# Gate products of a recurrent branch in two 64-row halves of TensorE, with ScalarE moving the input gates between halves

## The chip, the core and the metric

The kernel runs on one core of a Trainium2 chip. The metric is the device time of one execution in microseconds (us). TensorE (PE) multiplies a stationary matrix (`lhsT`, at most 128 rows by 128 columns) with a moving one and accumulates in PSUM; PEld is its loading of the stationary matrix. ScalarE (ACT), VectorE (DVE) and GpSimd (POOL) work element by element, and SyncE (SP) issues most of the transfers.

## The reference

A trunk of two layers on 256 positions of 1024 channels. Each layer mixes tokens by three branches (dilated attention, a gated linear recurrence, retention) and then retrieves experts. The change concerns the gates of the recurrence, `lx` being 1024 of the columns of the input projection:

```python
xc = lax.conv_general_dilated(lx, conv_w[:, None, :], ..., feature_group_count=LRU_WIDTH) + conv_b
xr = xc.reshape(B, S, LRU_BLOCKS, LRU_BLOCK_DIM)                       # 16 blocks of 64 channels
r = jax.nn.sigmoid(jnp.einsum('bsgi,gio->bsgo', xr, wa).reshape(B, S, C) + ba)
i = jax.nn.sigmoid(jnp.einsum('bsgi,gio->bsgo', xr, wx).reshape(B, S, C) + bx)
a = jnp.exp(-LRU_C * r * jax.nn.softplus(-lam))
b = jnp.sqrt(-jnp.expm1(2.0 * log_a)) * (i * xc)                        # h_t = a_t h_(t-1) + b_t
```

Both gate matrices are block diagonal: 16 blocks of 64 by 64, so a tile of 128 channels holds two blocks.

## The kernel before

All weights stream through the core as **jobs**: a job is one tile of 128 by 1024 float32. For each, SP loads `raw` (L220), ScalarE casts it to the high part `wh` (L239) and VectorE subtracts to get the low part `wl` (L256), so that three fast products (`xh` by `wh`, `xl` by `wh`, `xh` by `wl`) stand for one exact product. `run` works job by job: it first issues cast and subtraction of the job two ahead (`ensure_split(i + LA)`, `LA = 2`), then the products of job i (`body`), then a share of side work (`pump`), then what follows the job (`post`). Each engine executes in this order of issue.

The jobs of a layer are numbered here from 0: 0 to 7 give `lx` (a job is 24 products of 256 columns, with `wl` in the last eight, L307), 8 to 19 give the attention values `av` (12 products of 512 columns, L343, L344, L347, with `wl` from the fifth on), 20 to 43 the attention's queries and keys, and so on. After every second `lx` job, `post` copies the finished pair to `lx` in SBUF (L650, or L648 in layer 1's first pair); after jobs 11, 15 and 19, `post` copies `av` (L679, two copies).

Side work is written as generators whose yields are prices; `pump` resumes one while it has credit, and each job adds 1.4. The recurrence is one such queue ("lru"):

- `lru1`, once for each pair of channel tiles, four times in a layer. Two convolutions on VectorE (L583, L586), each priced 1.7. Then for each of the two tiles q a **gate group**: two products in full float32 (L594 and L595, each of which appears in the trace as two passes), two Tanh out of PSUM (L597, L598), a Tanh that makes log a (L599), and on VectorE the input gate times the convolution (L601), priced 0.5.
- `lru2`, once. Eight small operations (L610, L611), a square root over everything on ScalarE (L613), eight times a reciprocal on VectorE (L615) with two products on GpSimd, and eight times a product and a scan on VectorE (L620, L621).

The gate weights `wg` hold, for each gate and channel tile, a 128 by 128 matrix with two blocks on its diagonal and zeros elsewhere. Products of 64 rows exist elsewhere in the kernel: the attention scores (L710) multiply rows 0 to 63 and rows 64 to 127 alternately, each half into a PSUM bank of its own.

Of the kernel before, what the change touches and what calls it, by code (L numbers as in the profile page):

```python
# [11 lines left out]
F32 = mybir.dt.float32  # L12
# [3 lines left out]
AF = mybir.ActivationFunctionType  # L16
ALU = mybir.AluOpType
AX = mybir.AxisListType

S = 256  # L20
D = 1024
P = 128
KT = D // P
LAYERS = 2
# [139 lines left out]
def build(ctx: ExitStack, tc: tile.TileContext, I, out, layers=LAYERS, dbg=None):  # L164
    nc = tc.nc
    mm = nc.tensor.matmul
# [8 lines left out]
    par = cp.tile([P, LAYERS, 8, 12], F32, name="par")  # L175
# [7 lines left out]
    def nm(s):  # L183
        uid[0] += 1
        return f"{s}_{uid[0]}"
# [4 lines left out]
    def sideps():  # L190
        return ps.tile([P, 512], F32, tag="side", name=nm("side"), bufs=2)
# [364 lines left out]
    def mixer(l, mp, xdram, xnext):  # L556
        rope = mp.tile([P, 4, S], F32, name=nm("rope"), tag="rope")
        mask = mp.tile([P, 1152], F32, name=nm("mask"), tag="cst")
        wg = mp.tile([P, 2, 8, P], F32, name=nm("wg"), tag="L8", bufs=7)
        if l == 0:  # L560
            add_side("lru", init_lru(mp))

        def L8(shape=(P, 8, S), dt=F32):
            return mp.tile(list(shape), dt, tag="L8", name=nm("L8"), bufs=7)

        def w2():
            return mp.tile([P, 512], F32, tag="w2", name=nm("w2"), bufs=6)

        def pr(ct, k):
            return par[:, l, ct, k:k + 1]  # L570

        tT = L8()
        gi = L8()
# [3 lines left out]
        def lru1(c, lx):  # L577
            xcs = []
            for q in range(2):
                ct = 2 * c + q  # L580
                src = lx[:, q * S:(q + 1) * S]
                xc = mp.tile([P, S], F32, tag="xc", name=nm("xc"), bufs=3)
                nc.vector.tensor_scalar(xc, src, pr(ct, 3), pr(ct, 4), op0=ALU.mult, op1=ALU.add)  # L583
                for k in (2, 1, 0):
                    sh = 3 - k
                    nc.vector.scalar_tensor_tensor(xc[:, sh:], src[:, :S - sh], pr(ct, k), xc[:, sh:],  # L586
                                                   op0=ALU.mult, op1=ALU.add)
                xcs.append(xc)
                yield 1.7
            for q in range(2):  # L590
                ct = 2 * c + q
                xc = xcs[q]
                pg = sideps()
                mm(pg[:, 0:S], lhsT=wg[:, 0, ct, :], rhs=xc, start=True, stop=True)  # L594
                mm(pg[:, S:2 * S], lhsT=wg[:, 1, ct, :], rhs=xc, start=True, stop=True)  # L595
                tr = w2()
                nc.scalar.activation(tr[:, 0:S], pg[:, 0:S], AF.Tanh, bias=pr(ct, 5), scale=0.5)  # L597
                nc.scalar.activation(tr[:, S:2 * S], pg[:, S:2 * S], AF.Tanh, bias=pr(ct, 6), scale=0.5)  # L598
                nc.scalar.activation(tT[:, ct, :], tr[:, 0:S], AF.Tanh, bias=csp[:, l, ct:ct + 1],  # L599
                                     scale=csp[:, l, ct:ct + 1])  # L600
                nc.vector.scalar_tensor_tensor(gi[:, ct, :], tr[:, S:2 * S], 1.0, xc, op0=ALU.add, op1=ALU.mult)  # L601
                yield 0.5

        def lru2():
            sq = L8()
# [294 lines left out]
        m = L8((P, 2, D))  # L900
# [419 lines left out]
def inputs_for(x, w_in, conv_w, conv_b, lru_wa, lru_ba, lru_wx, lru_bx, lru_lambda, w_branch, w_out,  # L1320
# [11 lines left out]
    vecs = [ch(cw[:, k]) for k in range(4)] + [ch(a) for a in (conv_b, lru_ba, lru_bx, lru_lambda,  # L1332
                                                                        ln1_g, ln1_b, ln2_g, ln2_b)]
    A["par"] = f(np.stack(vecs, -1).transpose(2, 0, 1, 3))
    wg = np.zeros((LAYERS, P, 2, 8, P), np.float32)
    for m, w in enumerate((f(lru_wa), f(lru_wx))):
        for b in range(16):
            ct, o = divmod(b, 2)
            wg[:, o * 64:o * 64 + 64, m, ct, o * 64:o * 64 + 64] = w[:, b]
    A["wgate"] = wg  # L1340
    A["keys"] = f(np.stack([f(peer_k1), f(peer_k2)], 1).transpose(0, 4, 1, 2, 3))
    for n, a in (("ln1_g", ln1_g), ("ln1_b", ln1_b), ("ln2_g", ln2_g), ("ln2_b", ln2_b)):
# [18 lines left out]
```

## Time and profile before

| | us |
|---|---|
| median of the runs | 2494.98 |
| lowest | 2494.91 |
| the profiled execution | 2493.72 |
| its span, first to last instruction | 2491.9 |

| engine | busy us | share of the span |
|---|---|---|
| TensorE, products | 2464.3 | 99% |
| TensorE, loads of weights | 2245.0 | 90% |
| VectorE | 1834.6 | 74% |
| ScalarE | 1176.6 | 47% |
| GpSimd | 206.6 | 8% |

Products overlap in the pipeline, so the busy time of TensorE is not its time at peak. What a product costs in a stream is read from the distance between the starts of two neighbours.

### The profile page before, as it was taken

The page shows a single profiled execution, that of the slowest core. Times are in us where ns is not written, and L with a number is a line of the kernel's source. Part 1 is how long each engine was busy: PE and PEld are TensorE (multiplying, and loading weights), DVE is VectorE, ACT ScalarE, POOL GpSimd, SP SyncE. Part 2 cuts the span into 40 slices and gives each one's busy share as a digit, 9 for nine tenths or more (in the row PEclk, how much of TensorE's full clock was granted, in tenths as well). Part 3 has the DMA queues.
Part 4 walks back from the last instruction along what each step waited for, and adds up shares of the span by engine and source line. Part 5 has one row for each costly group of instructions (what it writes and reads, how often), then busy time and mean ns, then how long its engine had stood idle before and what let it go on. Part 6 is the DMA issues. An engine that isn't in the chain of part 4 may idle for free.

```text
span 2491.9 us, 41185 instructions
## 1 busy us (share of the span) xinstructions
PE 2464.3 (99%) x16404; PEld 2245.0 (90%) x16404; DVE 1834.6 (74%) x2732; ACT 1176.6 (47%) x1463; POOL 206.6 (8%) x195
## 2 busy tenths in 40 slices
PE   8999999999999999999999999999999999999998
PEld 7999988999999988888789999879999999888886
DVE  7976655889888856765679666578988888566656
ACT  5444444444444444444464444444454444444444
POOL 0512110100000000000015120110000000000000
PEclk9999999999999999999999999999999999999999
DMA  6544565655556558676565455656555565677664
GB/s 225 176 153 160 169 208 177 204 178 171 185 192 202 194 194 260 227 228 228 178 205 174 156 166 169 227 167 208 177 178 181 193 202 195 201 255 227 228 241 140
DMA packets 165904, 485.82 MB, mean 195 GB/s; under 512 B 15056, under 2 KB 47952, under 8 KB 165072
## 3 DMA queue, kind: packets, MB, share of 16 engines
q1 hardware_dynamic: 119952, 434.43, 53.2%
q10 hardware_dynamic: 44800, 45.62, 5.6%
q8 instruction: 129, 2.11, 0.3%
q0 software_dynamic: 960, 3.15, 0.3%
q14 instruction: 63, 0.52, 0.1%
HBM read 462.16 MB, written 20.97 MB: 194 GB/s over the span
## 4 chain that ended last, share of the span: by engine, by line
PE 97%; DVE 2%; issue 0%; ACT 0%; DMA 0%; POOL 0%; SPq 0%; ACTq 0%; DVEq 0%
PE acc L1259 28%; PE mm L304 15%; PE mm L305 15%; PE mm L307 15%; PE acc L343 6%; PE acc L344 6%; PE acc L347 6%; PE acc L1185 1%; PE acc L1186 1%; PE side L710 1%; PE side L1025 1%; PE side L766 0%; DVE wl L256 0%; PE acc L1250 0%; PE side L759 0%
## 5 line engine op out<-in xcount | busy, mean ns | idle before, releaser
L256 DVE TENSOR_TENSOR wl<-raw,wh 128x1024 fp32r<-128x1024 f32 (+1 forms) x811 | 1004.7, 1243 | 478.5 <-ACT wh L239 475.8
L239 ACT CAST wh<-raw 128x1024 fp32r<-128x1024 f32 (+1 forms) x817 | 851.7, 1050 | 639.7 <-PE acc L1259 343.1
L304 PE MATMUL mm<-xh,wh 128*128 128x256 f32 x3144 | 781.7, 286 | 0.0
L305 PE MATMUL mm<-xl,wh 128*128 128x256 f32 x3144 | 771.0, 283 | 0.0
L304 PEld LDWEIGHTS mm<-xh,wh 128*128 128x128 f32 x3144 | 602.5, 192 | 3.1 <-issue 2.6
L305 PEld LDWEIGHTS mm<-xl,wh 128*128 128x128 f32 x3144 | 603.3, 192 | 0.5
L1259 PE MATMUL acc<-wh,act 128*128 128x512 f32 x2016 | 539.3, 389 | 0.9 <-ACT act L351 0.9
L1259 PEld LDWEIGHTS acc<-wh,act 128*128 128x128 f32 x2016 | 378.4, 188 | 79.8 <-ACT act L351 1.3
L307 PE MATMUL mm<-xh,wl 128*128 128x256 f32 x3144 | 441.0, 283 | 0.0
L307 PEld LDWEIGHTS mm<-xh,wl 128*128 128x128 f32 x3144 | 405.6, 192 | 0.0
L1259 PE MATMUL acc<-wl,act 128*128 128x512 f32 x1008 | 310.2, 389 | 0.0
L1259 PEld LDWEIGHTS acc<-wl,act 128*128 128x128 f32 x1008 | 189.3, 188 | 39.2
L1228 ACT ACTIVATE ring<-mm 128x512 f32<-128x512 f32 x128 | 76.6, 599 | 189.6 <-PE mm L307 178.3
L343 PE MATMUL acc<-wh,xh 128*128 128x512 f32 x416 | 166.0, 399 | 0.0
L344 PE MATMUL acc<-wh,xl 128*128 128x512 f32 x416 | 162.3, 390 | 0.0
L347 PE MATMUL acc<-wl,xh 128*128 128x512 f32 x416 | 128.3, 390 | 0.0
L381 POOL TENSOR_TENSOR lnv<-lnv,mhalf 128x1 f32<-128x1 f32 x8 | 4.5, 558 | 1371.8 <-DVE lnv L378 1371.1
L1155 ACT ACTIVATE ge<-acc 128x512 f32<-128x512 f32 x64 | 38.4, 600 | 164.0 <-PE acc L1186 164.0
L343 PEld LDWEIGHTS acc<-wh,xh 128*128 128x128 f32 x416 | 78.2, 188 | 16.7 <-ACT r L853 0.7
L347 PEld LDWEIGHTS acc<-wl,xh 128*128 128x128 f32 x416 | 78.1, 188 | 16.7
L344 PEld LDWEIGHTS acc<-wh,xl 128*128 128x128 f32 x416 | 78.2, 188 | 15.5
L352 DVE TENSOR_TENSOR act<-ring,act 128x512 fp32r<-128x512 f32 x128 | 87.6, 685 | 3.8 <-ACT act L351 3.8
(245 smaller groups left out, 2225.9 us busy)
## 6 DMA issues: line engine op xcount, KB each, us to landing
raw<-in_ws SPq DMA_DIRECT2D x815, 512.0 KB, 3.4
gd<-ge ACTq DMA_DIRECT2D x64, 256.0 KB, 3.4
ring<-gd ACTq DMA_DIRECT2D x8, 2048.0 KB, 15.2
wg<-in_wgate SPq DMA_DIRECT2D x2, 1024.0 KB, 7.0
xd<-L POOLq DMA_DIRECT2D x8, 256.0 KB, 4.3
kk<-in_keys ACTq DMA_DIRECT2D x2, 1024.0 KB, 5.5
X<-xd ACTq DMA_DIRECT2D x2, 1024.0 KB, 5.8
dec<-in_dec ACTq DMA_DIRECT2D x2, 768.0 KB, 5.5
```

What stands on the lines that cost most here:

```text
L239: nc.scalar.copy(h[:, c], raw[:, c])
L256: e.tensor_tensor(lo[:, c], raw[:, c], h[:, c].bitcast(F32), op=ALU.subtract)
L304: mm(o, lhsT=w, rhs=mh[:, koff + k, :], start=(k == 0), stop=False)
L305: mm(o, lhsT=w, rhs=ml[:, koff + k, :], start=False, stop=False)
L307: mm(o, lhsT=lo[:, base + k * P:base + (k + 1) * P], rhs=mh[:, koff + k, :], start=False, stop=(k == n - 1))
L343: mm(acc[t], lhsT=sh[:, k, ts], rhs=h[:, q * 512:(q + 1) * 512], start=first, stop=False)
L344: mm(acc[t], lhsT=sl[:, k, ts], rhs=h[:, q * 512:(q + 1) * 512], start=False, stop=False)
L347: mm(acc[t], lhsT=sh[:, k, ts], rhs=lo[:, q * 512:(q + 1) * 512], start=False, stop=(last and q == 1))
L352: nc.vector.tensor_tensor(lo, src, h.bitcast(F32), op=ALU.subtract)
L1155: nc.scalar.activation(ge, pg.rearrange("p (k i) -> p i k", k=8)[:, 64:128, :], AF.Copy, scale=1.0 / GSCALE)
L1228: nc.scalar.activation(ring[s][:, i - 1:i + 1, :], pt.rearrange("p (a t) -> p a t", a=2), AF.Gelu)
L1259: mm(V["y"][t][n], lhsT=a[:, part, q, ts], rhs=w[:, n * 512:(n + 1) * 512], start=(j == 0 and x == 0), stop=False)
```

## The change

For a pair of channel tiles, the change makes four products of 64 rows by 128 columns (L596) where there were four of 128 by 128. Half b of the rows holds block b of a channel tile; its stationary matrix has that block of both gates side by side, so one product gives the recurrence gate and the input gate of the block. The output of half b goes to a PSUM bank of its own (`pg[b]`). In it, the recurrence gate of block b stands at the rows of block b, and the input gate at the rows of the other half. So the Tanh that reads an input gate writes to the other half (g against o in the diff), and each Tanh covers 64 rows: four for a channel tile where there were two. The two products with the convolution move behind a yield of their own, and the yields of `lru1` add up to 5.9 where they were 4.4. `wg` is half as large, and `xc` has four buffers for three.

```diff
-        wg = mp.tile([P, 2, 8, P], F32, name=nm("wg"), tag="L8", bufs=7)
+        wg = mp.tile([P, 8, P], F32, name=nm("wg"), tag="L8", bufs=7)
...
-                xc = mp.tile([P, S], F32, tag="xc", name=nm("xc"), bufs=3)
+                xc = mp.tile([P, S], F32, tag="xc", name=nm("xc"), bufs=4)
...
+            pg = [sideps(), sideps()]
+            for q in range(2):
+                for b in range(2):
+                    o = slice(64 * b, 64 * b + 64)
+                    mm(pg[b][:, q * S:(q + 1) * S], lhsT=wg[o, 2 * c + q, :], rhs=xcs[q][o, :], start=True, stop=True)
+            trs = []
             for q in range(2):
                 ct = 2 * c + q
-                xc = xcs[q]
-                pg = sideps()
-                mm(pg[:, 0:S], lhsT=wg[:, 0, ct, :], rhs=xc, start=True, stop=True)
-                mm(pg[:, S:2 * S], lhsT=wg[:, 1, ct, :], rhs=xc, start=True, stop=True)
                 tr = w2()
-                nc.scalar.activation(tr[:, 0:S], pg[:, 0:S], AF.Tanh, bias=pr(ct, 5), scale=0.5)
-                nc.scalar.activation(tr[:, S:2 * S], pg[:, S:2 * S], AF.Tanh, bias=pr(ct, 6), scale=0.5)
+                trs.append(tr)
+                for m in range(2):
+                    for b in range(2):
+                        o = slice(64 * b, 64 * b + 64)
+                        g = slice(64 * (b ^ m), 64 * (b ^ m) + 64)
+                        nc.scalar.activation(tr[o, m * S:(m + 1) * S], pg[b][g, q * S:(q + 1) * S], AF.Tanh,
+                                             bias=par[o, l, ct, 5 + m:6 + m], scale=0.5)
                 nc.scalar.activation(tT[:, ct, :], tr[:, 0:S], AF.Tanh, bias=csp[:, l, ct:ct + 1],
                                      scale=csp[:, l, ct:ct + 1])
-                nc.vector.scalar_tensor_tensor(gi[:, ct, :], tr[:, S:2 * S], 1.0, xc, op0=ALU.add, op1=ALU.mult)
-                yield 0.5
+            yield 1.5
+            for q in range(2):
+                nc.vector.scalar_tensor_tensor(gi[:, 2 * c + q, :], trs[q][:, S:2 * S], 1.0, xcs[q], op0=ALU.add,
+                                               op1=ALU.mult)
+            yield 1.0
```

Lines behind the change stand 12 later in the changed kernel (L608 is the Tanh of L599, L691 the copy of L679, L627 the reciprocal of L615, L725 the score scaling of L713).

On TensorE, layer 0, right behind job 4, the gate products of the first pair (side is the PSUM bank, xc the convolved tile):

```order
-L594 MATMUL side_344<-xc_270,wg_130 128x256
-L595 MATMUL side_344<-xc_270,wg_130 128x256
-L594 MATMUL side_352<-xc_305,wg_130 128x256
-L595 MATMUL side_352<-xc_305,wg_130 128x256
+L596 MATMUL side_344<-xc_270,wg_130 128x256
+L596 MATMUL side_345<-xc_270,wg_130 128x256
+L596 MATMUL side_344<-xc_305,wg_130 128x256
+L596 MATMUL side_345<-xc_305,wg_130 128x256
```

There are as many products as before, of the same number of moving columns, and neighbours now write to different banks. The later groups also change place: in layer 0 they stood behind jobs 7, 10 and 11, 13 and 14, and stand behind jobs 8, 12 and 17; in layer 1 they stood behind jobs 6, 9 and 12, and stand behind jobs 7, 11 and 15, which are jobs that `post` copies follow.

On ScalarE, layer 1, the third group of the change, with the cast of job 13 ahead of it and that of job 14 behind:

```order
L239 CAST wh_12987<-raw_12918 128x1024
L606 ACTIVATE w_1944_13009<-side_13003,par 64x256
L606 ACTIVATE w_1944_13009<-side_13004,par 64x256
L606 ACTIVATE w_1944_13009<-side_13003,par 64x256
L606 ACTIVATE w_1944_13009<-side_13004,par 64x256
L608 ACTIVATE L_1881_12602<-w_1944_13009,csp 128x256
L606 ACTIVATE w_1945_13015<-side_13003,par 64x256
L606 ACTIVATE w_1945_13015<-side_13004,par 64x256
L606 ACTIVATE w_1945_13015<-side_13003,par 64x256
L606 ACTIVATE w_1945_13015<-side_13004,par 64x256
L608 ACTIVATE L_1881_12602<-w_1945_13015,csp 128x256
L691 COPY av_13021<-acc_12924 128x512 x2
```

Before, the same place on ScalarE, with the copies of `av`, one cast, and then a gate group:

```order
L679 COPY av_13005<-acc_12907 128x512 x2
L239 CAST wh_13010<-raw_12925 128x1024
L597 ACTIVATE w_1954_13030<-side_13027,par 128x256
L598 ACTIVATE w_1954_13030<-side_13027,par 128x256
L599 ACTIVATE L_1881_12586<-w_1954_13030,csp 128x256
L597 ACTIVATE w_1956_13038<-side_13035,par 128x256
L598 ACTIVATE w_1956_13038<-side_13035,par 128x256
L599 ACTIVATE L_1881_12586<-w_1956_13038,csp 128x256
L239 CAST wh_13045<-raw_12959 128x1024
```

Four more Tanh stand in a group, and the two copies of `av` have moved from a place ahead of a cast of their own to one between a gate group and the next cast.

On VectorE, layer 0, from the subtraction of job 28 to that of job 30, before:

```order
L256 TENSOR_TENSOR wl_1003<-raw_890,wh_1002 128x1024
L620 SCALAR_TENSOR_TENSOR L_11_131<-L_11_131,L_97_665 128x256
L621 SCALAR_TENSOR_TENSOR L_96_664<-L_11_131,L_12_132 128x256
L713 SCALAR_TENSOR_TENSOR sm_1033<-side_1035,mask_129 128x384
L713 SCALAR_TENSOR_TENSOR sm_1034<-side_1036,mask_129 128x384
L256 TENSOR_TENSOR wl_1050<-raw_926,wh_1049 128x1024
L690 TENSOR_TENSOR w_157_1077<-mm_1006,rope_128 128x512
L691 TENSOR_TENSOR w_158_1078<-mm_1006,rope_128 128x512
L256 TENSOR_TENSOR wl_1086<-raw_960,wh_1085 128x1024
```

And in the change, the same jobs:

```order
L256 TENSOR_TENSOR wl_1010<-raw_894,wh_1009 128x1024
L725 SCALAR_TENSOR_TENSOR sm_1038<-side_1040,mask_129 128x384
L725 SCALAR_TENSOR_TENSOR sm_1039<-side_1041,mask_129 128x384
L256 TENSOR_TENSOR wl_1055<-raw_933,wh_1054 128x1024
L627 RECIPROCAL L_111_757<-L_111_757 128x256
L702 TENSOR_TENSOR w_157_1085<-mm_1013,rope_128 128x512
L703 TENSOR_TENSOR w_158_1086<-mm_1013,rope_128 128x512
L256 TENSOR_TENSOR wl_1094<-raw_967,wh_1093 128x1024
```

At job 28 the recurrence had reached its scans; in the change it is still at its reciprocals. Between the subtractions of job 23 and job 41 there were four reciprocals and seven pairs of product and scan, and there are seven and five.

## Rows read from the trace of the kernel before

**Rows 1.** The page: busy us by engine (share of the span), the chain that ended last.
```profile
PE 2464.3 (99%) x16404; PEld 2245.0 (90%) x16404; DVE 1834.6 (74%) x2732; ACT 1176.6 (47%) x1463; POOL 206.6 (8%) x195
...
PE 97%; DVE 2%; issue 0%; ACT 0%; DMA 0%; POOL 0%; SPq 0%; ACTq 0%; DVEq 0%
```
**Rows 2.** Waits of TensorE: line, releaser, us in total, times, longest.
```profile
PE side L594 <- DVE xc L586: 1.2, 2, 0.8
```
**Rows 3.** Timeline of TensorE, layer 0, second gate group: start us, us, engine, line, operation.
```profile
36.09 0.60 PE L594 MATMUL side<-xc,wg 128*128 128x256 f32 x2
...
38.05 0.40 PE L344 MATMUL acc<-wh,xl 128*128 128x512 f32 x1
```
**Rows 4.** The same, layer 0, second half of the first gate group.
```profile
26.48 0.70 PE L594 MATMUL side<-xc,wg 128*128 128x256 f32 x2 [0.39 <-DVE xc L586]
...
27.57 0.28 PE L305 MATMUL mm<-xl,wh 128*128 128x256 f32 x1
27.69 0.28 PE L304 MATMUL mm<-xh,wh 128*128 128x256 f32 x1
```
**Rows 5.** The same, layer 0, the 64-row attention scores behind job 26.
```profile
93.81 0.64 PE L307 MATMUL mm<-xh,wl 128*128 128x256 f32 x4
94.38 1.58 PE L710 MATMUL side<-qk 64*128 64x128 f32 x16
...
96.11 0.28 PE L305 MATMUL mm<-xl,wh 128*128 128x256 f32 x1
```
**Rows 6.** Line L710: count, duration in ns (min/median/max), first and last start, forms.
```profile
L710 PE MATMUL side<-qk x192: 272/374/378, 94.4 to 1425.8; 64*128 64x128 f32 x96, 64*128 64x256 f32 x96
```
**Rows 7.** Timeline of ScalarE, layer 1: a gate group, copies of av and a cast.
```profile
1283.56 0.47 ACT L597 ACTIVATE w<-side,par 128x256 f32<-128x256 f32 x1 [2.98 <-PE side L595]
1283.93 0.47 ACT L598 ACTIVATE w<-side,par 128x256 f32<-128x256 f32 x1
1284.29 0.60 ACT L599 ACTIVATE L<-w,csp 128x256 f32<-128x256 f32 x1
1284.78 0.47 ACT L597 ACTIVATE w<-side,par 128x256 f32<-128x256 f32 x1
...
1289.87 1.08 ACT L679 COPY av<-acc 128x512 f32<-128x512 f32 x2 [1.88 <-PE acc L347]
1290.83 1.07 ACT L239 CAST wh<-raw 128x1024 fp32r<-128x1024 f32 x1
```
**Rows 8.** Timeline of TensorE, layer 1, jobs 8 and 9, and a gate group.
```profile
1277.03 0.40 PE L343 MATMUL acc<-wh,xh 128*128 128x512 f32 x1
...
1277.96 0.62 PE L347 MATMUL acc<-wl,xh 128*128 128x512 f32 x2
...
1282.49 0.59 PE L594 MATMUL side<-xc,wg 128*128 128x256 f32 x2
```
**Rows 9.** Busy time of the engines in 72 to 150 us: PE, PEld, DVE, ACT, POOL, then the clock.
```profile
72.00:150.00 78.00, 78.00 (x646) 75.93 (x645) 77.25 (x87) 32.12 (x42) 39.13 (x34) 1.00 0.52 169
```
**Rows 10.** Lines of VectorE in that stretch: count, busy us, mean ns.
```profile
L615 DVE RECIPROCAL L<-L 128x256 f32<-128x256 f32 x7 | 12.2, 1738 | 0.0
L621 DVE TENSOR_TENSOR_SCAN L<-L,L 128x256 f32<-128x256 f32 x8 | 8.8, 1101 | 0.3
L620 DVE SCALAR_TENSOR_TENSOR L<-L,L 128x256 f32<-128x256 f32 x8 | 7.6, 955 | 0.0
```
**Rows 11.** Timeline of VectorE, layer 0: a reciprocal and what follows; job 41's subtraction.
```profile
78.51 1.74 DVE L615 RECIPROCAL L<-L 128x256 f32<-128x256 f32 x1
80.17 1.16 DVE L256 TENSOR_TENSOR wl<-raw,wh 128x1024 fp32r<-128x1024 f32 x1
...
140.35 1.21 DVE L256 TENSOR_TENSOR wl<-raw,wh 128x1024 fp32r<-128x1024 f32 x1
```
**Rows 12.** Timeline of TensorE: job 41's products with its low part.
```profile
142.59 1.12 PE L307 MATMUL mm<-xh,wl 128*128 128x256 f32 x8
```
**Rows 13.** Lines of GpSimd in 60 to 160 us: a product of lru2, mean 1250 ns.
```profile
L617 POOL TENSOR_TENSOR L<-L,L 128x256 f32<-128x256 f32 x8 | 10.0, 1250 | 4.2 <-DVE L L615 4.0
```

More of the change, by code (lines that the diff above doesn't have):

```diff
@@ L1334, in inputs_for @@
     A["par"] = f(np.stack(vecs, -1).transpose(2, 0, 1, 3))
-    wg = np.zeros((LAYERS, P, 2, 8, P), np.float32)
+    wg = np.zeros((LAYERS, P, 8, P), np.float32)
     for m, w in enumerate((f(lru_wa), f(lru_wx))):
@@ L1338, in inputs_for @@
             ct, o = divmod(b, 2)
-            wg[:, o * 64:o * 64 + 64, m, ct, o * 64:o * 64 + 64] = w[:, b]
+            c = 64 * (o ^ m)
+            wg[:, o * 64:o * 64 + 64, ct, c:c + 64] = w[:, b]
     A["wgate"] = wg
```

## Prediction

> **What bounds the kernel now.** I read the page first: TensorE is busy for 2464.3 us, 99% of the span, and the chain of work that ended last runs 97% over TensorE [rows 1]. So a product saved anywhere in the stream is saved at the end, unless TensorE then arrives at something that is not ready. Next, the waits: at the gates it loses 1.2 us, in two places, one in each layer, where the second convolution of the first pair is late [rows 2]. Elsewhere the gate products follow their neighbours without a gap, and their price is the distance between the starts around them [rows 3]. Last, who is nearly late. From 72 to 150 us VectorE is busy 77.25 of 78.00 us, and TensorE still never waits, at a granted clock of 1.00 [rows 9]. Casts and subtractions are made two jobs ahead, so a burst on ScalarE may last about two jobs before TensorE feels it. The sum is therefore a gain on TensorE less what ScalarE and VectorE take back.
>
> **The gain on TensorE.** A full gate group of four products runs from 36.09 us to the start of the next job. That job's second product starts at 38.05, and neighbours of its kind are 0.23 apart (four from 1277.03 to 1277.96) [rows 3, 8], so the group costs 38.05 - 0.23 - 36.09 = 1.73 us: eight passes of 0.216.
>
> The changed form does not stand in the gates of the trace, but it stands in the scores: 64 rows, two halves, two banks, full float32. One score group is 16 passes, half of 256 and half of 128 moving columns [rows 6]. The job before it ends at 93.81 + 4 x 0.12 = 94.29 and the next begins at 96.11 - 0.12 = 95.99 (0.12 is the distance 27.57 to 27.69) [rows 4, 5], so the group costs 1.70 us. One after the other the passes would take 8 x 0.216 + 8 x 0.108 = 2.59 us, in pairs 1.30. So pairs do run side by side, and entering and leaving the 64-row form costs the other 0.40. The Trainium skill (TensorEngine Tiling (Array Packing), Theoretical Speedup) allows "Up to 2×" for a dimension of at most 64; by that alone a group would cost 0.87 and eight groups save 6.9 us. The same page (Key Properties) says that a change of tiling mode drains the engine and gives no price; the 0.40 of the scores agrees, and I take the row.
>
> A changed group then costs 4 x 0.216 + 0.40 = 1.27 us and saves 0.46. There are eight groups. Six run without a wait, also those of layer 0 that stood as two halves behind different jobs (each half costs half). They save 6 x 0.46 = 2.76. The other two are the first of each layer, where TensorE waits for the second convolution whatever the products cost. From that point the old half takes 27.57 - 0.12 - 26.48 = 0.97 [rows 4], which is 0.86 of passes and 0.11 of a first load that nothing hides. The new half takes 0.43 + 0.11 + half of the 0.40 (leaving) = 0.74, and saves 0.23; two save 0.46. Gain: **3.2 us**. The bounds: 6.9 if the switch cost nothing, and a loss of 3.2 (8 x 0.40) if the pairs ran one after the other.
>
> **What ScalarE takes back.** A group held four Tanh from PSUM and two of L599; it holds eight and two. No row shows a Tanh on 64 rows or one that moves between halves. The nearest is that on 128 rows: it follows its neighbour after 0.37 or 0.36 us, and what follows L599 does so after 0.49 (1284.29 to 1284.78) [rows 7]. I take these, since the elements along a row are as many as before; the bounds are half (0.18), if rows counted, and 0.49, that of the Tanh with the longest distance. The burst is 2 x (0.37 + 3 x 0.36 + 0.49) = 3.88 us, against 2 x (0.37 + 0.36 + 0.49) = 2.44. It starts when the last gate product ends, about when TensorE goes on with the next job. Queued behind it on ScalarE are what `post` issues and then the cast of the job two further on; that job's subtraction (1.22) waits for the cast, and TensorE for the subtraction.
>
> Between `av` jobs TensorE comes to that `wl` after two jobs, 1282.49 - 1277.03 = 5.46 us, plus 0.93 (1277.03 to 1277.96) in which it needs the high part only [rows 8]: 6.39. ScalarE and VectorE get there:
> - with nothing between (layer 0, behind jobs 8 and 12): 3.88 + 1.07 + 1.22 = 6.17, 0.22 to spare;
> - with the two copies of `av` between, 0.96 from their start to the cast's (layer 1, jobs 11 and 15) [rows 7]: 3.88 + 0.96 + 1.07 + 1.22 = 7.13, late by 0.74, twice;
> - with the copy of `lx`, one of that size (layer 1, job 7): 6.65, late by 0.26.
>
> Behind job 17, and behind the first group of each layer, the job concerned needs its `wl` only in its last third; nothing is late. Together **1.7 us**, all in layer 1. Bounds: 0 at half a Tanh. At 0.49 the burst is 1.02 longer, the five places cost 2 x 0.80 + 1.28 + 2 x 1.76 = 6.4, and the sum turns into a loss.
>
> **What VectorE takes back.** Its instructions are as many as before, but `lru1` is priced 1.5 more for each pair, so `lru2` starts four to five jobs later. In layer 0 the least slack of the saturated stretch is at job 41: the subtraction ends at 140.35 + 1.21 = 141.56 and is used at 142.59, 1.03 later [rows 11, 12]. Between jobs 23 and 41 the change has three reciprocals more, 1.66 each from start to start (78.51 to 80.17), and two pairs of product and scan fewer, 2.06 each [rows 10, 11]: 0.9 us more work. TensorE comes 1.6 us earlier (one group of 0.23, three of 0.46). Against that, reciprocals that stood ahead of job 23 are gone from there. The subtraction of job 23 then waits for its cast alone, which stands behind the square root; I estimate 1.2 us earlier, bounds 0 and 1.6. Slack: 1.03 - 0.9 - 1.6 + 1.2 = -0.27, so 0.3 us at most is lost (1.5 at the low bound). I take **0.2**. In layer 1 TensorE arrives no earlier by my sum, and I take nothing.
>
> **At nothing.** The smaller `wg` saves 512 KB of transfer in each layer; no wait hangs on it, since the gates wait for the convolution [rows 2]. The input-gate products on VectorE stand behind a yield more, where their Tanh is done. The later GpSimd products of `lru2` fall between the rotary ones, whose scores come two jobs later; if that cover were gone, scores would wait for one of 1.25 us [rows 13], three times in a layer.
>
> **Sum.** 3.2 - 1.7 - 0.2 = 1.3 us less. The profiled execution took 2493.72 (its span and 1.8 us around), so 2492.4; the median of the runs stands 1.3 above it, at 2494.98. I predict 2493.7.
>
> **Rivals.**
> - *ScalarE is not late.* If a Tanh of 64 rows were shorter, or the burst started early, only the 3.2 us would count, less 0.2: 2492.0. Against it, the distance of 0.36 already is much shorter than the duration of 0.47 [rows 7], so pipelining is in the sum.
> - *The other side: a Tanh between halves is slower.* From 0.41 us a Tanh on the gain is used up (8 x 0.043 = 0.34 more in each burst, 1.7 in the five places, less the spare 0.44, beside the 1.7 + 0.2 above); at 0.49 it is 3.2 - 6.4 - 0.2, a loss of 3.4: 2498.4. The place is ScalarE between a gate group and the next cast. For it speaks that no row shows this form; against it, that only start partitions differ. The Trainium skill (TensorEngine Tiling (Array Packing), PSUM Bottleneck) warns of this kind of turn: tiling quickens TensorE and not the emptying of PSUM, which may become the bound. Here it could in the layers' `av` jobs alone.
> - *The halves do not run side by side.* Then each group costs 1.73 + 0.40, and with ScalarE's 1.7 the time is 2494.98 + 3.2 + 1.7 = 2499.9. The scores speak against it [rows 5].
> - *The switch is free where the groups are short.* The gain is 6.9, less 1.9: 2490.0.
>
> **How the numbers follow.** The forecast 0.60, with 2492.5 to 2495 as its own range; ScalarE not late 0.20; slower Tanh 0.10; halves one after the other 0.05; free switch 0.05. From 2490.5 to 2498.5 lie 0.90 of these. Two per cent of this kernel is 50 us, about what a measurement can tell from no change; every case lies within a tenth of that. Faster by over 2%: 0.01; within 2%: 0.97; slower: 0.02, for a wait that I have not seen.
>
> **What would show it.** Right: L596 in pairs that start within some ns of each other, and groups of about 1.27 us; Tanh of L606 0.36 apart; new waits of TensorE in layer 1 for L256 or L239 behind jobs 7, 11 and 15, some 0.2 to 0.8 us each; none there in layer 0; a wait of some tenths at job 41 at most. Wrong: L596 starts 0.2 apart one by one; L606 0.45 apart or more; waits at the scores for GpSimd, or for L256 at several jobs between 24 and 43.

## The result, and the profile after

The change made the kernel slower: 2511.17 us (median; 2510.26 to 2512.04) against 2494.91 measured together with it, a ratio of 1.0066 with a 95% interval of 1.0055 to 1.0078. One execution in five of each kernel took over 4060 us (that of the change at a mean granted clock of 0.556) and is left out of this range and of the ratio, though not of the medians. Against the bound of 2% the result is no change, as forecast, but the forecast was a gain of 1.3 us, and the time lies 12.7 us above the predicted range and above the highest rival (2499.9). The profiled execution took 2512.04 us, 18.3 more than that of before; its span is 2510.3 against 2491.9.

The page first: TensorE has nearly the busy time of before [rows 1], and its share falls by a point.

```profile
PE 2468.8 (98%) x16404; PEld 2239.8 (89%) x16404; DVE 1830.1 (73%) x2732; ACT 1194.0 (48%) x1495; POOL 202.0 (8%) x195
```

So TensorE waits. Its waits (line, releaser, us in total, times, longest), which answer to [rows 2]:

```profile
PE side L596 <- DVE xc L586: 8.6, 7, 1.4
...
PE acc L343 <- ACT wh L239: 4.2, 5, 1.3
```

Seven of the eight gate groups now wait for a convolution of VectorE, where two waited before, 1.2 us in all. On TensorE's timeline in layer 0, the second group (answering to [rows 3]) and the fourth, the only one without a wait:

```profile
39.59 0.70 PE L596 MATMUL side<-xc,wg 64*128 64x256 f32 x4
41.74 0.70 PE L596 MATMUL side<-xc,wg 64*128 64x256 f32 x4 [1.45 <-DVE xc L586]
42.37 0.50 PE L343 MATMUL acc<-wh,xh 128*128 128x512 f32 x1
...
71.36 0.61 PE L347 MATMUL acc<-wl,xh 128*128 128x512 f32 x2
71.90 1.13 PE L596 MATMUL side<-xc,wg 64*128 64x256 f32 x8
72.97 0.50 PE L343 MATMUL acc<-wh,xh 128*128 128x512 f32 x1
73.31 0.40 PE L344 MATMUL acc<-wh,xl 128*128 128x512 f32 x1
```

The fourth group, counted as in the prediction, takes 73.31 - 0.23 - 71.90 = 1.18 us from its first start. That start comes 0.08 later than a third product at distance 0.23 would (71.36 + 0.46 = 71.82), so the group costs 1.26. The second is held 1.45 us between its two channel tiles. What ScalarE does behind that group, answering to [rows 7]:

```profile
37.43 1.05 ACT L239 CAST wh<-raw 128x1024 fp32r<-128x1024 f32 x1
42.47 1.94 ACT L606 ACTIVATE w<-side,par 64x256 f32<-64x256 f32 x4 [3.98 <-PE side L596]
44.43 0.60 ACT L608 ACTIVATE L<-w,csp 128x256 f32<-128x256 f32 x1
...
47.39 2.93 ACT L239 CAST wh<-raw 128x1024 fp32r<-128x1024 f32 x3
```

Two things are to be seen. Four Tanh of 64 rows take 44.43 - 42.47 = 1.96 us from start to start, 0.49 each (0.37 and 0.36 before), and the burst lasts 47.39 - 42.47 = 4.92 us. And it starts at 42.47, after the products of **tile 1** (41.74), though tile 0's had run from 39.59: ScalarE sat idle for 3.98 us. In the kernel before, the Tanh of tile 0 did not wait for tile 1. There its first group, in which TensorE also waits for tile 1's convolution (its products start at 26.48 [rows 4]), shows on ScalarE:

```profile
26.14 0.47 ACT L597 ACTIVATE w<-side,par 128x256 f32<-128x256 f32 x1 [2.21 <-PE side L595]
...
28.88 1.04 ACT L239 CAST wh<-raw 128x1024 fp32r<-128x1024 f32 x1
```

Last, VectorE between the first two groups of after:

```profile
26.91 1.22 DVE L256 TENSOR_TENSOR wl<-raw,wh 128x1024 fp32r<-128x1024 f32 x1
33.76 1.22 DVE L256 TENSOR_TENSOR wl<-raw,wh 128x1024 fp32r<-128x1024 f32 x1 [5.63 <-ACT wh L239]
34.91 0.75 DVE L612 SCALAR_TENSOR_TENSOR L<-w,xc 128x256 f32<-128x256 f32 x2
...
36.71 0.40 DVE L583 TENSOR_SCALAR xc<-w,par 128x256 f32<-128x256 f32 x1
...
40.16 1.52 DVE L586 SCALAR_TENSOR_TENSOR xc<-w,par,xc 128x255 f32<-128x255 f32 x3
```

This closes a ring. VectorE stands idle for 5.63 us for a cast that waits behind the first burst, which lasts from 27.79 to 32.70:

```profile
32.70 1.03 ACT L239 CAST wh<-raw 128x1024 fp32r<-128x1024 f32 x1
```

The convolutions stand behind that subtraction in VectorE's order and end at 40.16 + 1.52 = 41.68. The gate products start at 41.74, the next burst after them at 42.47. So what delays a burst delays the next one too.

Where the 18.4 us of span lie I worked out by comparing the distances from start to start of TensorE's products, product for product, in the two traces; a product directly behind a gate group, in either kernel, is counted with the groups:

| stretch | gate groups, us | other products, us |
|---|---|---|
| layer 0, `lx` and `av` | +3.84 | +0.98 |
| layer 0, attention | 0 | +3.09 |
| layer 1, `lx` and `av` | +3.96 | +5.07 |
| start, norms and the rest | 0 | +1.4 |

Of the last line, 0.58 and 0.63 us lie around two places in the norms where the clock of TensorE fell (last section).

### The profile page after: what moved, and what is told of

The parts are those of the page before. It is cut to its first block, busy times and chain, and to the rows that moved or that the text cites. A ratio compares the mean times of both kernels' runs of the same rounds, so it can differ in the third digit from the quotient of the medians.

```text
span 2510.3 us, 41208 instructions
## 1 busy us (share of the span) xinstructions
PE 2468.8 (98%) x16404; PEld 2239.8 (89%) x16404; DVE 1830.1 (73%) x2732; ACT 1194.0 (48%) x1495; POOL 202.0 (8%) x195
## 5 line engine op out<-in xcount | busy, mean ns | idle before, releaser
L304 PE MATMUL mm<-xh,wh 128*128 128x256 f32 x3144 | 781.6, 286 | 1.7 <-ACT wh L239 0.9
L304 PEld LDWEIGHTS mm<-xh,wh 128*128 128x128 f32 x3144 | 602.3, 192 | 6.5 <-issue 3.3
L343 PE MATMUL acc<-wh,xh 128*128 128x512 f32 x416 | 165.9, 399 | 4.2 <-ACT wh L239 4.2
L343 PEld LDWEIGHTS acc<-wh,xh 128*128 128x128 f32 x416 | 78.1, 188 | 24.8 <-ACT wh L239 6.3
```

The costliest lines, as they stand in the source:

```text
L304: mm(o, lhsT=w, rhs=mh[:, koff + k, :], start=(k == 0), stop=False)
L343: mm(acc[t], lhsT=sh[:, k, ts], rhs=h[:, q * 512:(q + 1) * 512], start=first, stop=False)
```

## The experiments

Four theories, in the words of the expectations: **T1**, the price of a Tanh of 64 rows; **T2**, place and prices of the generator `lru1` (yields of 5.9 for 4.4, both tiles' products at one place); **T3**, the products of 64 rows, or the way across halves; and, formed after e10, **T4**, two tiles in one PSUM bank. The table gives the times; each ratio is to the kernel before as measured together with the run (2494.91 us for after, 2494.45 for e1 to e4, 2494.78 for e5, e6, e7 and e10, 2494.44 for the others):

| run | products | Tanh rows | generator | banks | us | ratio, 95% interval |
|---|---|---|---|---|---|---|
| after | 64 | 64 | new | shared | 2511.17 | 1.0066 (1.0055 to 1.0078) |
| e1 | 128 | 64 | old | own | 2499.24 | 1.002 (1.0008 to 1.0031) |
| e2 | 64 | 128 | new | shared | 2494.36 | 0.9998 (0.9987 to 1.001) |
| e3 | 128 | 128 | new | own | 2495.96 | 1.0007 (0.9996 to 1.0019) |
| e4 | 64 | 64, other order | new | shared | 2510.95 | 1.0067 (1.0044 to 1.009) |
| e5 | 64 | 64 | new, a step more | shared | 2504.02 | 1.0039 (1.0025 to 1.0053) |
| e6 | 64 | 64, tiles adjacent | new | shared | 2507.28 | 1.0051 (1.0034 to 1.0067) |
| e7 | 64 | 64 | old yields | shared | 2512.14 | 1.0072 (1.0055 to 1.0088) |
| e10 | 128 | 64 | new | own | 2503.68 | 1.0036 (1.0022 to 1.005) |
| e13 | 64 | 64, burst split | new, a step more | shared | 2500.71 | 1.0025 (1.0015 to 1.0034) |
| e14 | 128 | 64 | new | shared | 2512.73 | 1.0072 (1.0055 to 1.0088) |
| e15 | 64 | 64 | new | own | 2501.32 | 1.0026 (1.0017 to 1.0036) |
| e16 | 64 | 128 | new | own | 2493.65 | 0.9997 (0.9987 to 1.0006) |

### One part of the change at a time

**e1: the kernel before with each Tanh in two of 64 rows.**

```diff
-                nc.scalar.activation(tr[:, 0:S], pg[:, 0:S], AF.Tanh, bias=pr(ct, 5), scale=0.5)
-                nc.scalar.activation(tr[:, S:2 * S], pg[:, S:2 * S], AF.Tanh, bias=pr(ct, 6), scale=0.5)
+                order = ((0, 0), (0, 1), (1, 0), (1, 1)) if q == 0 else ((0, 0), (1, 0), (0, 1), (1, 1))
+                for m, b in order:
+                    o = slice(64 * b, 64 * b + 64)
+                    nc.scalar.activation(tr[o, m * S:(m + 1) * S], pg[o, m * S:(m + 1) * S], AF.Tanh,
+                                         bias=par[o, l, ct, 5 + m:6 + m], scale=0.5)
```

> The kernel before, with one thing changed: each Tanh out of PSUM is split into two of 64 rows, each reading and writing the same half. In even channel tiles neighbours alternate between halves, in odd tiles two on half 0 come before two on half 1. The result is the same. Theory T1 (the price of a 64-row Tanh: neighbours no longer overlap, the burst makes casts late, subtractions and convolutions queue behind): Tanh about 0.49 us apart as in the changed kernel, bursts of about 4.9 us for 2.44, and 8 to 18 us more than before. If only alternating halves stops the overlap, the odd tiles show 0.36 between neighbours of one half. Theory T2 (the place: the new prices of the generator put the gates where their convolution is late): at most 2 us more than before. Theory T3 (the 64-row products themselves): no change.

Measured: 2499.24, 4.8 us slower: more than T2 allowed (2) and less than T1 expected (8 to 18). ScalarE's timeline of one burst (L600 the Tanh, L602 what was L599):

```profile
37.27 1.93 ACT L600 ACTIVATE w<-side,par 64x256 f32<-64x256 f32 x4 [3.15 <-PE side L595]
39.23 0.60 ACT L602 ACTIVATE L<-w,csp 128x256 f32<-128x256 f32 x1
39.84 1.68 ACT L600 ACTIVATE w<-side,par 64x256 f32<-64x256 f32 x4
41.55 0.60 ACT L602 ACTIVATE L<-w,csp 128x256 f32<-128x256 f32 x1
```

Tile 0, whose neighbours change the half each time, takes 39.23 - 37.27 = 1.96 us; tile 1, which stays in a half for two, 1.71. The single starts are 0.47 to 0.50 us apart where the half changes, and 0.373 where it stays, the distance of 128 rows. So it is the change of half from one Tanh to the next that lengthens the distance, not the 64 rows, and not the way across halves, which no Tanh takes here. Twice as many Tanh at 0.37 would make a burst of 3.9 us; the rest of after's 4.9 is the change of half.

**e2: after with Tanh of 128 rows**, which leaves out moving the input gates between halves.

```diff
-                    for b in range(2):
-                        o = slice(64 * b, 64 * b + 64)
-                        g = slice(64 * (b ^ m), 64 * (b ^ m) + 64)
-                        nc.scalar.activation(tr[o, m * S:(m + 1) * S], pg[b][g, q * S:(q + 1) * S], AF.Tanh,
-                                             bias=par[o, l, ct, 5 + m:6 + m], scale=0.5)
+                    nc.scalar.activation(tr[:, m * S:(m + 1) * S], pg[m][:, q * S:(q + 1) * S], AF.Tanh,
+                                         bias=pr(ct, 5 + m), scale=0.5)
```

> The changed kernel with Tanh on 128 rows: one for each gate and tile reads a whole bank. That leaves out moving the input gates between halves (the gates of some channels are exchanged); products, prices and order stay. T1: the burst falls to 2.44 us, the waits of TensorE for the convolutions and the casts go but for the first group of each layer, and the time is 2491 to 2494, at or a little under the kernel before. T2: the waits stay, 2508 to 2511. T3: the same as T2.

Measured: 2494.36, 0.36 above what T1 expected; the whole loss is gone, with products of 64 rows, the new prices and the shared banks still there, and the waits for `xc` are 2.8 us in four places. Without the longer Tanh there is no loss (T1).

**e3: the kernel before with the new prices and order**, products and Tanh of 128 rows, a bank for each tile. Against before:

```diff
+            pgs = [sideps(), sideps()]
+            for q in range(2):
+                ct = 2 * c + q
+                mm(pgs[q][:, 0:S], lhsT=wg[:, 0, ct, :], rhs=xcs[q], start=True, stop=True)
+                mm(pgs[q][:, S:2 * S], lhsT=wg[:, 1, ct, :], rhs=xcs[q], start=True, stop=True)
...
-                yield 0.5
+            yield 1.5
...
+            yield 1.0
```

> The kernel before with the changed prices and order of the generator (both gate groups of a pair, then 1.5, the two products with the convolution, then 1.0; four xc buffers), but with its 128-row products and 128-row Tanh. The result is the same. T1: 2494 to 2497, no wait of TensorE for a convolution but the first of each layer. T2: 2505 to 2513, with the seven waits for the convolutions. T3: as T1.

Measured: 2495.96, and L594 waits 1.4 us for `xc` in two places, nearly as before. T2 alone is worth some 1.5 us, within its interval nothing. In its trace 1.77 us are lost in the attention of layer 0.

**e4: after with another order of the Tanh.**

```diff
-                for m in range(2):
-                    for b in range(2):
+                for m, b in ((0, 0), (1, 1), (0, 1), (1, 0)):
```

> The changed kernel with its four Tanh of a tile in another order, so that each shares its input half or its output half with the one before: in 0 out 0, in 0 out 1, in 1 out 1, in 1 out 0. The result is the same. If a shared input half lets neighbours overlap, the first and third step are 0.36 us and the second and fourth 0.49; if a shared output half does, the second; if 64 rows alone forbid it, all stay at 0.49 and the time stays at 2510 to 2512. With two steps of four at 0.36 the burst is 0.5 us shorter and the time some 3 us less.

Measured: 2510.95, as after. Neighbours now share the half they read or the half they write, never both, and start 0.48 to 0.50 us apart. Between two of these Tanh it takes both to get 0.37. The bursts are 4.75 to 4.88 us long, since the Tanh of a whole tile behind the fourth one follows after 0.375 (last section).

Alone, Tanh in halves costs 4.8 us and the prices 1.5; together with the products they cost 16.3. Some 10 us were still without a cause.

### What makes the rest

**e5: after, with a step between convolutions and gate products.**

```diff
+            yield 1.4
             pg = [sideps(), sideps()]
```

> The changed kernel with one more step between a generator's convolutions and its gate products, so that a projection's products and casts lie between them. Theory T1 with the ring (the burst of Tanh delays ScalarE's casts, these VectorE's subtractions and convolutions, and TensorE's gate products, which come right behind, wait for the convolutions): the waits of gate products for xc, 8.6 us in seven groups, fall below 2 us, the burst stays 4.9 us long and the waits for casts (wh) stay; about 2502 to 2505 us. Rival T2 (the loss lies in the burst's total length on ScalarE, wherever the waits surface): the waits move from xc to wh, and the time stays at 2509 to 2512 us. Rival T3 (products of 64 rows): gate groups stay at 2.7 us.

Measured: 2504.02, as T1 with the ring expects. No wait of the gate products for `xc` is left in the list of waits; those for casts are (L343 for `wh`, 3.0 us, five times). Part is given back in the attention: `lru1` ends later, and L304 waits 2.7 us for VectorE there, in both layers.

**e6: after, with the two tiles adjacent for each gate and half.**

```diff
-            for q in range(2):
-                for m in range(2):
-                    for b in range(2):
+            for m in range(2):
+                for b in range(2):
+                    for q in range(2):
```

> The changed kernel with the Tanh of 64 rows ordered so that the two tiles of a block stand next to each other: four of the eight neighbours in a burst share the input's half and the output's half. If a change of half alone ends the overlap of ScalarE's neighbours: starts 0.373 us apart within such a pair and 0.48 across, a burst of about 4.3 us in place of 4.9. The time by proportion (2494.4 us with a burst of 2.2 us, 2511.2 with 4.9: 6.2 us for each us of burst): about 2507 us. If the loss has a threshold below 4.3 us: 2509 to 2511. If place and prices of the generator make the loss (T2): no change, 2511.

Measured: 2507.28. Distances within a pair are 0.37, across 0.47 to 0.48; the burst is 45.75 - 41.34 = 4.41 us, 0.5 less than in after:

```profile
41.34 3.38 ACT L603 ACTIVATE w<-side,par 64x256 f32<-64x256 f32 x8 [3.82 <-PE side L596]
...
45.75 1.03 ACT L239 CAST wh<-raw 128x1024 fp32r<-128x1024 f32 x1
```

That takes 3.9 us off the time, nearly all of eight bursts by 0.5: hardly anything hides a burst of this length any more. The executions of each kernel lie within 1.8 us, but the intervals of the two ratios overlap.

**e7: after with the old generator.**

```diff
+                nc.vector.scalar_tensor_tensor(gi[:, ct, :], tr[:, S:2 * S], 1.0, xcs[q], op0=ALU.add, op1=ALU.mult)
+                yield 0.5
-            yield 1.5
-            for q in range(2):
-                nc.vector.scalar_tensor_tensor(gi[:, 2 * c + q, :], trs[q][:, S:2 * S], 1.0, xcs[q], op0=ALU.add,
-                                               op1=ALU.mult)
-            yield 1.0
```

> The changed kernel with the old place and prices of the generator (Tanh and gi of a tile, then 0.5, then the next tile), products of 64 rows and Tanh across halves as in the changed kernel. The interplay of about 10 us which neither Tanh in halves alone (+4.8 us) nor the prices alone (+1.5 us) gives: if it is Tanh with the changed prices, 2498 to 2501 us here; if it is Tanh with the products of 64 rows, or the way across halves, 2508 to 2512 us.

Measured: 2512.14. I read it as T3, the branch that the expectation offered, and that was wrong, as e14 shows: e7 shares its banks too. Nor does it clear the prices, since two more things differ in its trace. The products of both tiles still stand together, and VectorE now comes to the product with the convolution while the Tanh still run. From 20 to 75 us it waits 11.8 us for them, where in after it never does (before: 4.2 us, for L598):

```profile
DVE L L610 <- ACT w L606: 11.8, 8, 2.0
```

And the gate products wait 10.8 us for `xc` in eight groups. Behind the three longest of these waits (2.22 us before 39.49, 2.06 before 52.88, 2.15 before 1308.52) TensorE's granted clock falls to the lower level, as here behind the second (busy us of PE, PEld, DVE, ACT and POOL, then the clock):

```profile
54.00:56.00 2.00, 2.00 (x7) 1.52 (x6) 0.41 (x1) 1.91 (x5) 0.00 (x0) 0.50 0.39 143
```

The products there start 0.42 us apart in place of 0.23. Compared product for product with before, each fall costs about 1.5 us, some 4.5 of the 17.4 that e7 loses; no other run has such a fall in the recurrence. All four executions of e7 have a mean granted clock of 0.995 or 0.996, those of the other experiments 0.997 to 0.999. What the prices are worth inside the change stays open.

**e10: the other side, e3 with Tanh in halves**, none of them across.

```diff
-                    nc.scalar.activation(tr[:, m * S:(m + 1) * S], pgs[q][:, m * S:(m + 1) * S], AF.Tanh,
-                                         bias=pr(ct, 5 + m), scale=0.5)
+                    for b in range(2):
+                        o = slice(64 * b, 64 * b + 64)
+                        nc.scalar.activation(tr[o, m * S:(m + 1) * S], pgs[q][o, m * S:(m + 1) * S], AF.Tanh,
+                                             bias=par[o, l, ct, 5 + m:6 + m], scale=0.5)
```

> The kernel before with the changed place and prices and with each Tanh in two of 64 rows that alternate the half (burst about 4.7 us), products of 128 rows and no way across halves. The other side of the run with the old prices: if the interplay is Tanh with the changed prices, 2507 to 2511 us (the groups of gate products wait for xc some 8 us in all); if it is Tanh with products of 64 rows or the way across halves, about 2501 us (4.8 and 1.5 us added to 2494.5).

Measured: 2503.68, between the two values, nearer to 2501. TensorE and ScalarE at one group:

```profile
52.16 0.59 PE L594 MATMUL side<-xc,wg 128*128 128x256 f32 x2
52.59 0.59 PE L595 MATMUL side<-xc,wg 128*128 128x256 f32 x2
54.29 0.67 PE L594 MATMUL side<-xc,wg 128*128 128x256 f32 x2 [1.10 <-DVE xc L586]
```
```profile
53.23 1.93 ACT L603 ACTIVATE w<-side,par 64x256 f32<-64x256 f32 x4 [1.56 <-PE side L595]
...
58.26 1.04 ACT L239 CAST wh<-raw 128x1024 fp32r<-128x1024 f32 x1
```

Here tile 0's Tanh starts at 53.23, before tile 1's products (54.29) and 1.07 us after its own. In after it came behind tile 1's. What differs is not the rows but the bank: after puts both tiles into `pg[b][:, q * S:...]`. That made T4.

**e14: e10 with shared banks and nothing else changed** (the Tanh read `pgs[m][o, q * S:...]` accordingly).

```diff
-                mm(pgs[q][:, 0:S], lhsT=wg[:, 0, ct, :], rhs=xcs[q], start=True, stop=True)
-                mm(pgs[q][:, S:2 * S], lhsT=wg[:, 1, ct, :], rhs=xcs[q], start=True, stop=True)
+                mm(pgs[0][:, q * S:(q + 1) * S], lhsT=wg[:, 0, ct, :], rhs=xcs[q], start=True, stop=True)
+                mm(pgs[1][:, q * S:(q + 1) * S], lhsT=wg[:, 1, ct, :], rhs=xcs[q], start=True, stop=True)
```

> The run with halves and prices (products of 128 rows, 2503.7 us) with one thing changed: the two tiles of a block share their two PSUM banks, as in the changed kernel (bank m holds gate m of both tiles, where it was one bank for each tile). Theory T4: the first Tanh of a burst waits for the last product written to the bank it reads, so sharing makes the Tanh of tile 0 wait for the convolution and the products of tile 1, as in the changed kernel, where it starts 0.41 us after the last product of the group and not 0.41 us after the last of its own tile. Then the first Tanh comes 2.5 to 3.3 us after the first product where the convolution of tile 1 is late (1.06 in the run with halves and prices), each block's burst ends about 1.4 us later, and the time is 2509 to 2514 us. Rival T3 (products of 64 rows, or the way across halves, make the rest of the loss): 2503 to 2505 us.

Measured: 2512.73, with products of 128 rows and no way across halves. The same group:

```profile
54.34 0.59 PE L594 MATMUL side<-xc,wg 128*128 128x256 f32 x2
54.77 0.59 PE L595 MATMUL side<-xc,wg 128*128 128x256 f32 x2
56.39 0.70 PE L594 MATMUL side<-xc,wg 128*128 128x256 f32 x2 [1.02 <-DVE xc L586]
56.92 0.59 PE L595 MATMUL side<-xc,wg 128*128 128x256 f32 x2
```
```profile
57.12 1.93 ACT L603 ACTIVATE w<-side,par 64x256 f32<-64x256 f32 x4 [3.28 <-PE side L594]
...
62.14 1.03 ACT L239 CAST wh<-raw 128x1024 fp32r<-128x1024 f32 x1
```

The first Tanh waits for L594 of tile 1, which writes the bank that it reads, and not for L595 (56.92 to 57.51), which writes the other. It comes 57.12 - 54.34 = 2.78 us after the first product, 1.7 later than in e10, and the next cast 7.80 after it (6.10 in e10).

**e15: after with banks of its own for tile 1.**

```diff
-            pg = [sideps(), sideps()]
+            pgs = [[sideps(), sideps()], accps2() if pos[0] <= 8 else [mmps(), mmps()]]
             for q in range(2):
+                pg = pgs[q]
...
+                pg = pgs[q]
```

> The changed kernel, with products of 64 rows and Tanh across halves, in which tile 1 of a block has two banks of its own (of the acc banks in the first eight jobs, of the mm banks after them). T4: the first Tanh starts about 0.75 us after the first product wherever the convolution of tile 1 stands, and the time falls to 2499 to 2503 us (the run with halves and prices, 2503.7, less up to 0.47 us in each of eight groups). Rival T3: the time stays at 2509 to 2512 us.

Measured: 2501.32. The first Tanh again goes ahead of tile 1:

```profile
51.11 0.70 PE L597 MATMUL side<-xc,wg 64*128 64x256 f32 x4
53.00 0.70 PE L597 MATMUL mm<-xc,wg 64*128 64x256 f32 x4 [1.19 <-DVE xc L586]
```
```profile
51.85 1.94 ACT L608 ACTIVATE w<-side,par 64x256 f32<-64x256 f32 x4 [1.32 <-PE side L597]
```

So sharing costs 9.4 us with either kind of product, each run taken against its own kernel before (e14 18.3 and e10 8.9; after 16.3 and e15 6.9). The Trainium skill (PSUM — Partial Sum Buffer, PSUM bank collisions raise a hardware error) says why the wait can't simply be dropped: another engine must not touch a bank, in the same quadrant of rows, that TensorE is writing, and PSUM is to be guarded by bank and quadrant (in the simple version by bank), not by address. The traces agree in that ScalarE came behind tile 1 only where the bank was shared; no run here lets the two collide. Each buffer of these products fills a bank, so no run tells a wait for the bank from one for the buffer.

**e13: after with a step between the Tanh of tile 0 and tile 1.**

```diff
+                if q == 0:
+                    yield 1.4
             yield 1.5
```

> The changed kernel with a step between the Tanh of tile 0 and those of tile 1, so that a job's cast stands between two bursts of 2.45 us. If it is the length of one unbroken burst that delays the casts (T1 and the ring): the waits for casts fall and the time is 2497 to 2502 us. If ScalarE's total work decides: 2504 to 2511 us. The gate products still come right behind the convolutions, so their waits for xc go only as far as the ring slackens: under 5 us of 8.6.

Measured: 2500.71, in the range of the length of one unbroken burst; the waits for casts are gone from the list, and those for `xc` fall to 5.0 us. A cast now stands in the middle:

```profile
43.80 1.95 ACT L606 ACTIVATE w<-side,par 64x256 f32<-64x256 f32 x4 [3.96 <-PE side L596]
...
46.28 1.03 ACT L239 CAST wh<-raw 128x1024 fp32r<-128x1024 f32 x1
47.22 1.92 ACT L606 ACTIVATE w<-side,par 64x256 f32<-64x256 f32 x4
```

ScalarE does the same work as in after; the place of a cast in it and a generator that lasts one step longer together make 10 us. The run does not part the two: e5, with a step as long in another place and the burst unbroken, gives 7 of them, so the break itself is worth 3 us if a step gives the same in both places.

**e16: e2 with the banks of e15** (the two edits shown there together), the most that this change could bring.

> The changed kernel with Tanh of 128 rows (which leaves out moving the input gates between halves; 2494.4 us so) and with own banks for tile 1: what the products of 64 rows can bring where neither Tanh nor a shared bank stands behind them. T4: below that run, 2490.5 to 2493.5 us. If the shared bank costs nothing with a short burst: 2494 us again.

Measured: 2493.65, ratio 0.9997 (0.9987 to 1.0006), 0.15 us above the expected range. With a short burst the shared bank makes 0.7 us between the medians (e2, e16), and even with both costs taken away the products of 64 rows show no gain that these runs can tell from none. No run here is faster than the kernel before beyond its interval.

## Why the prediction was wrong, point by point

- **The price of the products was right.** Pairs start some 7 ns apart, and the undisturbed group costs 1.26 us (predicted 1.27). The total gain, 3.2 in the sum, can't be told from that or from nothing: e10 to e15 and e14 to after, which differ in the products and in the way across halves (with bursts 0.1 to 0.2 us shorter for it), give 2.0 us each, and e3 to e16, which differ in the products alone, 2.3, but the intervals of these runs are 2.4 to 4.1 us to either side.
- **"Six run without a wait" failed.** It was read from the trace of before as if it were a property of the groups. It holds only as long as VectorE is early there. In after seven of eight wait, and 8.6 us are lost to `xc` where before lost 1.2; to a growth of this wait the sum gave no term.
- **The Tanh was mis-sized.** Taken at 0.36 to 0.37 us, measured at 0.47 to 0.50; the burst is 4.92 us and not 3.88. The prediction had the right price at the right place among its rivals (slower Tanh, 0.49, chance 0.10), and refused it with "against it, that only start partitions differ". That difference is the cause, though not as a way between halves: in e1 every Tanh stays in its half and is as slow where its neighbour was in the other. Yet at 0.49 the rival gave 2498.4, and the kernel took 2511.2; so the size of this term was not the main failure.
- **"It starts when the last gate product ends" hid the new wait.** True of after, but in before a tile's burst starts when that tile's products end. The shared bank makes tile 0 wait for tile 1's convolution. The prediction asked what stands behind the burst and never what stands ahead of it. This is worth 9.4 us with the long burst (e14, e15), and 0.7 with a short one (e2, e16).
- **ScalarE's term was followed one step only.** From burst to cast to subtraction to TensorE's `wl`. The other way out of VectorE was left out: the convolutions stand behind the same subtraction, and the next gates, and so the next burst, behind them. Once such a chain closes, it sets the pace, and what is added is paid nearly in full in each turn: between e2 (burst 2.4 us, with the slack still there) and after (4.9) eight bursts grew by 20 us in all, and 16.8 arrived at the end; between e6 and after 4.1, of which 3.9 arrived. The prediction passed on 1.7 us of the 11.5 by which it let the eight bursts grow. It is this step, together with the bank, that failed. Of the waits it did forecast, those for casts and subtractions in layer 1, "1.7 us" became 5.07 in the table above.
- **VectorE's term was right at its place and too short.** At job 41 0.22 us are lost (predicted 0.2). That the size agrees is luck: two stops just ahead of it, where before had 135.9 and 137.4 us, lose 0.64 and 0.90 (the second mostly a wait for ScalarE, L304 for `p`), and job 23 loses 0.86, with the products around them 3.09 us in all. With the old generator (e1, e7) there is none of it, with the new one alone (e3) 1.77. So it is T2's, and the Tanh add to it.

- **What stays open.** The loss adds up as 4.8 (e1) and 1.5 (e3), 2.6 by which e10 is above their sum, 9.4 for the shared banks, less 2.0 between e14 and after: 16.3 us. The 2.6 are not explained by a run; in the traces about half of them lies in layer 0's attention, where e10 loses 3.04 us, e3 1.77 and e1 nothing. The table's last line, 1.4 us, is in part scatter: the start alone differs by -0.6 to +0.5 us between these runs.

## What to carry to other kernels

When results of two products were put into one PSUM bank here, the first reader waited for the last product written to it: look for what the last writer waits for, before counting banks saved. When an engine's burst grows, follow it through every instruction queued behind it on every engine, until the chain ends or comes back to the burst; if it comes back, each delay is paid once a turn, nearly in full here. Then two things help beside shortening the burst (3.9 us for half a us less in e6): letting its first half start early (9.4 us), and a cast in its middle with a step more between the bursts (10 us). And a group that never waits in a trace has slack of unknown size, which has to be measured from the releaser's end, not taken from the absence of a wait.

## What the runs showed of the hardware

**ScalarE's neighbours overlap only where the halves stay.** Two Tanh of 64 rows start 0.37 us apart when the second reads and writes the halves of the first, and 0.47 to 0.50 when the half of input or output changes (e1, e4, e6), where the duration of one is 0.47. The Trainium skill (ScalarE: Activation LUTs, What ACT_TABLE_LOAD costs) says that neighbours overlap by about 93 ns; these traces agree where the halves stay (0.47 - 0.37 = 0.10), and show about none where they change. The Tanh of whole tiles between them fit one pattern: an instruction comes late when it writes at another half than the last one, or reads PSUM at another half than the last one that read PSUM, a whole tile counting as one that starts at the first half. In e4 the fourth Tanh writes the first half, and L607 follows after 0.375; in after it writes the second, and L608 follows after 0.48 to 0.49. The next Tanh out of PSUM then comes 0.60 later in e4, where the last read of PSUM was at the other half, and 0.51 in after, where it was at the same. The pattern was read from the traces afterwards; no run was made to test it, and none shows why.

**The clock fell at the same waits in one trace and not in the other.** Behind waits of TensorE of 2.2 and 2.1 us in the norms of the two layers its granted clock was 0.50, the lower level (1.2 GHz), in two stretches of after; behind waits of 2.1 and 2.2 us at the same places in before it stayed at 1.00. Windows of after and of before (PE, PEld, DVE, ACT, POOL, then the clock):

```profile
448.00:450.00 2.00, 2.00 (x10) 2.00 (x11) 1.96 (x6) 2.00 (x6) 1.85 (x1) 0.50 0.39 139
1698.00:1700.00 2.00, 2.00 (x11) 2.00 (x11) 1.93 (x5) 2.00 (x5) 1.65 (x3) 0.50 0.38 74
```
```profile
440.00:442.00 2.00, 2.00 (x20) 2.00 (x19) 1.97 (x6) 2.00 (x6) 1.82 (x2) 1.00 0.31 111
```

In two us TensorE starts 10 or 11 products for 20; around the two places after is 0.58 and 0.63 us longer. The traces of the experiments show one to five such falls each (the last microseconds left out), at the norms but for the three in e7. What decides whether the clock falls stays open.
